# Six-row tiles in four slots, and a first tile loaded whole, in a max-pool-and-subtract kernel

## The chip, the cores and the metric

The kernel runs on one core of one Trainium2 chip. The time is device microseconds (us). Runs of a kernel agree within some 0.03 to 1% (626.60 to 626.78 us in eleven runs of the kernel before), so small differences are judged from repeated rounds beside the kernel before on the same chip.

## The reference

```python
def reference(x):                                   # x: 8 x 64 x 256 x 256 float32
    x_r = x.reshape(B, C, oH, 8, oW, 8)
    pooled = x_r.max(axis=(3, 5))                   # max of each 8 x 8 window
    upsampled = np.repeat(np.repeat(pooled, 8, axis=2), 8, axis=3)
    return (x - upsampled).astype(np.float32)
```

134.22 MB come in, as many go out. A "row" below is 2048 elements (8 lines of 256, 8 KB): the unit that can be pooled alone. There are 128 x 128 of them; a tile of n rows gives each of the 128 partitions n rows in succession.

## The kernel before

One buffer, the ring, holds `SLOTS` tiles of `SIZE` rows. Loads are issued by SyncE (queue q1), stores by ScalarE (queue q10); VectorE pools each tile and subtracts in place. The load of a tile waits for the store of the tile that last had its slot. TensorE only turns "loaded" into one semaphore for the loop.

```python
HEAD, HEAD_OUT = [2, 2], [2, 2]     # first tile: rows per load, rows per store
SIZE, TILES = 5, 24
TAIL = [2, 1, 1]                    # last tile: rows per pooling and store
SLOTS = 5
...
for i in range(len(sizes)):                                     # loads
    slot = slot_of(i)
    if landed[slot]:
        nc.sync.wait_ge(stored[slot], 16 * landed[slot])
    for k, (lo, R) in enumerate(cuts(HEAD if i == 0 else [sizes[i]])):
        nc.sync.dma_start(out=sbuf(i, lo, R), in_=dram(x_rows, i)[:, part]).then_inc(
            first[k] if i == 0 else loaded[slot], 16)
...
for i in range(len(sizes)):                                     # stores
    for lo, R in cuts(HEAD_OUT if i == 0 else TAIL if i == last else [SIZE]):
        ...
        nc.scalar.wait_ge(ready, done)
        nc.scalar.dma_start(out=dram(out_rows, i)[:, part], in_=sbuf(i, lo, R)).then_inc(...)
...
def pool_and_subtract(part, top, R, nth=None):                  # VectorE
    nc.vector.tensor_reduce(out=maxs, in_=..., axis=XY, op=max).then_inc(...)
    ...
    for r in range(R):
        sub = nc.vector.tensor_tensor(out=wins[:, r], in0=wins[:, r], in1=<maxs[:, r] broadcast>, op=subtract)
    sub.then_inc(ready, 1)
```

## Time and profile before

| | before |
|---|---|
| time, median of 3 runs | 626.66 us (626.66 to 626.77) |
| span of the profiled run | 624.8 us |
| bytes | 268.44 MB |
| VectorE busy | 90% |
| DMA engines, loads + stores | 49.9% + 49.7% |
| transfers | 27 loads, 29 stores |

How to read it: two nearly full resources and a clear order between them. The DMA engines are busy all the time; in the steady part VectorE has a gap of about 2.1 us in each turn (a turn is one pass of its loop, one tile), in which it waits for a load. The prediction below shows the lines and the working.

### The profile page before, as it was taken

The numbers are of one execution on the slowest core, as the hardware profiler recorded it, in microseconds if no ns is written. First come the engines' busy times: TensorE is split into PE (matmuls) and PEld (weight loads), VectorE is DVE, ScalarE is ACT, GpSimd is POOL, SyncE is SP. The second block draws the span as 40 slices with busy tenths as digits, with TensorE's granted clock in tenths as the row PEclk, the third lists the DMA queues.
The fourth block names the chain that finished last, engine by engine and source line by source line (L and its number), as shares of the span: only waits on it lengthen the run. The fifth ranks groups of instructions, "written<-read, shape, count | busy, mean of one in ns | idle before, by whom it ended". The sixth has DMA issues, their size and how long they took to land. (4 is left out here: it accounts for less than half of the span.)

```text
span 624.8 us, 557 instructions
## 1 busy us (share of the span) xinstructions
DVE 561.1 (90%) x157; POOL 0.2 (0%) x4
## 2 busy tenths in 40 slices
DVE  4899999999989889898898898898898898988992
POOL 0000000000000000000000000000000000000000
DMA  9999999999999999999999999999999999999998
GB/s 366 406 457 441 420 420 461 420 420 461 420 420 461 420 420 461 420 420 461 420 420 461 420 420 461 420 420 461 420 420 461 420 420 459 422 422 442 450 422 352
DMA packets 8064, 268.44 MB, mean 430 GB/s; under 512 B 896, under 2 KB 896, under 8 KB 896
## 3 DMA queue, kind: packets, MB, share of 16 engines
q1 hardware_dynamic: 3888, 134.22, 49.9%
q10 hardware_dynamic: 4176, 134.22, 49.7%
HBM read 134.22 MB, written 134.22 MB: 430 GB/s over the span
## 5 line engine op out<-in xcount | busy, mean ns | idle before, releaser
L81 DVE TENSOR_REDUCE tops<-ring (+2 forms) x29 | 277.4, 9566 | 47.9 <-DVEq L75 39.6
L96 DVE TENSOR_TENSOR ring<-ring,tops (+1 forms) x128 | 284.4, 2285 | 3.9 <-DVEq L75 3.7
L165 POOL MEMSET const-bfloat16-1.0<- 128x1 bf16 x1 | 0.1, 102 | 0.0
L165 POOL MEMSET const-uint8-127<- 128x1 uint8 x1 | 0.1, 102 | 0.0
L165 POOL MEMSET const-float32-0.0<- 128x1 f32 x1 | 0.1, 99 | 0.2 <-issue 0.2
L165 POOL MEMSET const-float32-1.0<- 128x1 f32 x1 | 0.1, 99 | 0.0
## 6 DMA issues: line engine op xcount, KB each, us to landing
ring<-in_x_dram SPq DMA_DIRECT2D x24, 5120.0 KB, 57.6
out_dram<-ring ACTq DMA_DIRECT2D x24, 5120.0 KB, 40.7
out_dram<-ring ACTq DMA_DIRECT2D x3, 2048.0 KB, 20.9
ring<-in_x_dram SPq DMA_DIRECT2D x2, 2048.0 KB, 9.6
ring<-in_x_dram SPq DMA_DIRECT2D x1, 4096.0 KB, 55.1
out_dram<-ring ACTq DMA_DIRECT2D x2, 1024.0 KB, 11.8
```

The source lines that it names most:

```text
L81: nc.vector.tensor_reduce(out=maxs if R > 1 else maxs[:, 0], in_=(wins.rearrange("p r ph ow pw -> p r ow ph pw") if R > 1 else wins[:, 0]. ...
L96: sub = nc.vector.tensor_tensor(out=wins[:, r], in0=wins[:, r], in1=maxs[:, r].unsqueeze(1).unsqueeze(3).to_broadcast([P, pH, oW, pW]), op ...
L165: nc = _bacc.Bacc("TRN2", target_bir_lowering=False, num_devices=1)
```

## The change

Its intent: fewer, larger transfers, and a simpler head. 24 rows of ring take the place of 25; the first tile of four rows comes in one load, is pooled and stored in halves.

```diff
-HEAD, HEAD_OUT = [2, 2], [2, 2]
-SIZE, TILES = 5, 24
+HEAD, HEAD_OUT = [4], [2, 2]
+SIZE, TILES = 6, 20
 TAIL = [2, 1, 1]
-SLOTS = 5
+SLOTS = 4
...
-        for k, (lo, R) in enumerate(cuts(HEAD)):
-            nc.vector.wait_ge(first[k], 16)
+        for k, (lo, R) in enumerate(cuts(HEAD_OUT)):
+            nc.vector.wait_ge(first[[a + n >= lo + R for a, n in cuts(HEAD)].index(True)], 16)
             pool_and_subtract(sbuf(0, lo, R), top(0, lo, R), R, k + 1)
```

(The rest is the bookkeeping of the same counts.)

More of the change, by code (lines that the diff above doesn't have):

```diff
@@ L127 @@
                 part = slice(lo * ROW, (lo + R) * ROW)
-                done = [sum(HEAD[: k + 1]) for k in range(len(HEAD))].index(lo + R) + 1 if i == 0 else done + 1
+                done += 1
                 nc.scalar.wait_ge(ready, done)
@@ L149 @@
         for k, (lo, R) in enumerate(cuts(TAIL)):
-            pool_and_subtract(sbuf(last, lo, R), top(last, lo, R), R, len(HEAD) + k + 1)
+            pool_and_subtract(sbuf(last, lo, R), top(last, lo, R), R, len(HEAD_OUT) + k + 1)
 _INS = ['x']
```

## The prediction

Its sum came to 626.2 us: from the 626.66 measured, one small term for the nine fewer transfers was taken off, and the rest was rounded towards the change. The 28.9 us near the end still has the term in it.

Three terms in it need their basis. "Packet-wise turns" is the assumption that the 16 engines serve loads and stores in turn, a packet each. The records of the kernel before fit it: while the 256 store packets of 16 KB of the first tile passed (21.69 to 53.35 us), 240 load packets of 40 KB started, 70% of the bytes, where 5/7 is 71%. The 2.6 us beside the bytes are measured; "1.5 of completion" is an estimate of their later part. In the records the last increment of the first load comes 0.35 us after its last packet, that of the first tile's second store 1.80 us after (55.15 us). And the fifth of the five-row loads was released there, at 55.16 us in the trace, where the text reads "near 54" from the wait.

> **What bounds the kernel now.** I read four views in this order: the busy shares, the DMA queues, the stretches, and the waits of the DMA-issuing queues. First the page itself.
>
> ```profile
> span 624.8 us, 557 instructions
> ...
> DVE 561.1 (90%) x157; POOL 0.2 (0%) x4
> ...
> DMA packets 8064, 268.44 MB, mean 430 GB/s; under 512 B 896, under 2 KB 896, under 8 KB 896
> ...
> q1 hardware_dynamic: 3888, 134.22, 49.9%
> q10 hardware_dynamic: 4176, 134.22, 49.7%
> ```
>
> Loads (q1) and stores (q10) take 49.9% and 49.7% of the time of all 16 DMA engines: 99.6% together. VectorE is busy for 90%. So the DMA engines are the bound and VectorE is close behind. Next, the stretches (stretch, its length, busy time of VectorE and of GpSimd, clock, share of the DMA engines, GB/s):
>
> ```profile
> 0.00:2.00 2.00, 0.00 (x0) 0.20 (x4) 1.00 0.16 33
> 2.00:18.00 16.00, 9.61 (x4) 0.00 (x0) 1.00 1.02 422
> 18.00:53.00 35.00, 32.83 (x10) 0.00 (x0) 1.00 0.99 419
> ...
> 185.85:572.96 387.11, 350.69 (x96) 0.00 (x0) 1.00 1.00 434
> ...
> 595.00:613.00 18.00, 17.83 (x8) 0.00 (x0) 1.00 0.96 414
> 613.00:623.00 10.00, 0.00 (x0) 0.00 (x0) 1.00 0.95 403
> 623.00:625.00 2.00, 0.00 (x0) 0.00 (x0) 1.00 0.00 0
> ```
>
> The fourth line is exactly 16 turns of the loop, from the start of one reduce to the start of another. 387.11/16 = 24.194 us a turn, in which five rows per partition come in and five go out: 2 x 5,242,880 B / 24.194 us = 433.4 GB/s. All 268.44 MB at that rate would take 619.4 us; the span is 624.8. Only 5.4 us (0.9%) lie outside the steady rate: about 2 us before the first packet, 1.8 us after the last (nothing moves after 623), and some 1.5 us of slightly lower rate in the head and the tail. The timeline of VectorE shows that it waits in the steady part, not the DMA engines:
>
> ```profile
> 548.89 10.82 DVE L81 TENSOR_REDUCE tops<-ring  x1 [2.17 <-DVEq L75]
> 559.86 11.10 DVE L96 TENSOR_TENSOR ring<-ring,tops  x5 [0.15 <-DVEq L75]
> 572.96 10.82 DVE L81 TENSOR_REDUCE tops<-ring  x1 [2.00 <-DVEq L75]
> ```
>
> Each turn starts with about 2.1 us of waiting for a load. Without that wait a turn takes 21.98 us (the starts at 50.13 and 72.11, early in the same timeline).
>
> [...] The trace: the first load of 2.10 MB was issued at 0.94 and released VectorE at 8.36, 7.4 us; less 4.8 us at 433.4 GB/s leaves 2.6[...].
>
> **The change part by part.**
>
> *Bytes.* None is removed: 134.22 MB in, 134.22 MB out. At a saturated 433.4 GB/s this alone keeps the sum at 619.4 us.
>
> *Number of transfers.* Before: 27 loads (2+24+1) and 29 stores (2+24+3). After: 1+20+1 = 22 loads and 2+20+3 = 25 stores. Nine fewer of 56. Packets are one per partition plus 16 small ones for each transfer (27 x 144 = 3888 and 29 x 144 = 4176, as the queues show), so 3168 and 3600 are to be seen. What is one worth?[...] If transfers were wholly free of cost, 0.
>
> *VectorE.* A reduce costs 2.28 us for one row, 4.41 for two, 10.82 for five: 2.135 a row and about 0.14 fixed. Six rows: 12.95. The 29 reduces become 25 (20 of six rows, three of two, two of one): 276.8 us against 277.4. The 128 subtracts stay. A turn without waiting becomes 21.98 x 6/5 less a share of the fixed part, 26.3 us. A saturated turn becomes 24.194 x 6/5 = 29.03[...]. So VectorE still waits 2.6 to 2.7 us a turn, and gains nothing that reaches the end.
>
> *Head.* The first load is 4.19 MB whole. VectorE starts at 0.94 + 2.6 + 4.19 MB/433.4 = 13.2 us instead of 8.36, and the first store is issued near 22.1 instead of 17.34. This 4.8 us is a delay of VectorE, not of the DMA engines: four more loads of 22 rows in all (4 + 3 x 6) stand in the queue from the start, some 53 us of work at 2.42 us a row (1.049 MB at 433.4).
>
> *Ring.* 24 rows instead of 25, and only three full tiles ahead of the first wait for a store. Is the load queue ever empty with no store at hand? The first store packets are 16 KB, while load packets are 40 KB before and 48 KB after, and by the packet-wise turns the loads get 5/7 and 3/4 of the engines. Check on the kernel before: at 18.3 us, when the first store's packets begin, (18.3 - 1.9)/2.42 = 6.8 rows have come in; the tile's four stored rows then pass beside ten loaded ones, 14 x 2.42 = 33.9, so at 52.2 plus 1.5 of completion the queue of loads is released, near 53.7. The waits of the load queue say:
>
> ```profile
> SPq L113 <- DMA out_dram<-ring: 51.3, 1, 51.3
> ```
>
> This is the view up to 60 us; the wait starts near 3 us after the six first issues, so it ended near 54. The rule holds. After: stores begin near 23.2 us with 8.8 rows in; four stored rows pass beside twelve loaded ones, to 61.9 us, with 20.8 of the 22 rows in. The fifth load is released near 63.5, with about one row left to load and the next six-row store (issued near 57.5) already queued. So the loads nearly run out there, but the engines have store work, and nothing is lost. Carried on by hand, VectorE is behind the loads until about its ninth tile (near 240 us; before it was the seventh, 161.65) and each store lands some 50 us after issue, each load some 35 to 40. Both sums fit the ring: four turns of 29.0 are 116, of which VectorE holds 26.3, so load and store latency and waits must fill 89.7. Before it was 57.6 + 40.7 + 22.
>
> *Tail.* The last four rows are cut as before. When the last load lands (594.3 before: issued 539.2, 55.1 to landing), about 28 us of stores remain, so the end is a drain of stores. VectorE's last 18 us lie beside it. After, a backlog of stores of about four rows (10 us) plus six plus four rows remains, and VectorE finishes its last full tile some 2 to 7 us after that landing. The drain should stay unbroken.
>
> *Sum.* 626.66[...] + 0 (head, under the queue) + 0 (ring) + 0 (tail), and I round towards the change: **626.2 us**.
>
> **The rivals.** (1) *The ring starves.* With four slots both queues could be empty while VectorE works on a six-row tile. Against it: the latencies above sum to three turns, so there is a turn or more of queued work at any time. For it: the load queue gets within some 4 us of empty, and the estimate of the tail leaves only a few us. If 0.5 us were lost in each of 20 turns the time would be 636. Likelier is one gap of 2 to 3 us at the end, 628 to 629. (2) *VectorE becomes the bound.* Its work after the start is 561 us and it starts 4.8 us later; 13.2 + 561 + about 4 of gaps = 578, well before 613. It could be late by some 35 us without effect. Only if its chain fell behind in the drain would it show. (3) *Bigger packets move the rate itself*, 48 KB against 40.[...] (4) *The head gains*, since the first packets are 32 KB, not 16 KB: the stretch 2 to 18 ran at 422 and not 434; all of it back would be 0.4 us.
>
> **Range and chances.** The bound is untouched, and every term is under 1 us unless a queue runs dry.[...] a loss is open-ended, but needs both queues empty. So 624.8 to 628.2 for 8 in 10. Faster by over 2% would need under 614[...]: 0.01. Slower by over 2% needs 12.5 us of idle DMA engines: 0.02. The rest, 0.97, is the same.
>
> **What would show it.** Packets of 3168 and 3600; six-row reduces of 12.95 us; a turn of 28.9 to 29.0 us with 2.6 of waiting; the first reduce near 13.2; the load queue's first wait about 61 us; DMA share of 1.00 in all stretches between 2 and 620; stores that land later than before and loads sooner. Wrong would be a stretch with a share clearly below 1, a turn away from 29.0, or a gap between the last stores.

## The result, and the profile after

The changed kernel takes 626.57 us (median of 6 runs, 626.44 to 627.03); the kernel before took 626.71 in the same rounds. The ratio is 0.9999, with a 95% interval of 0.9986 to 1.0012: the same. Ratios here are the mean time of one kernel's runs over that of the other's of the same rounds, so not quite the ratio of the medians. Executions over 1.5% slower than the fastest of the same kernel are left out of the means.

The page of the changed kernel:

```profile
span 625.3 us, 516 instructions
...
DVE 559.9 (90%) x153; POOL 0.2 (0%) x4
...
q1 hardware_dynamic: 3168, 134.22, 49.8%
q10 hardware_dynamic: 3600, 134.22, 49.6%
...
L81 DVE TENSOR_REDUCE tops<-ring (+2 forms) x25 | 276.8, 11071 | 44.5 <-DVEq L75 31.5
```

The packets are the 3168 and 3600 that were predicted, and the DMA engines are as full as before. The stretches (length, VectorE, GpSimd, clock, DMA share, GB/s):

```profile
186.00:307.00 121.00, 112.55 (x31) 0.00 (x0) 1.00 1.00 432
307.00:428.00 121.00, 109.69 (x29) 0.00 (x0) 1.00 1.00 435
...
595.00:613.00 18.00, 12.61 (x6) 0.00 (x0) 1.00 0.96 413
613.00:623.00 10.00, 0.00 (x0) 0.00 (x0) 1.00 0.93 396
```

The tail is as it was. One steady stretch is a little lower than the others, and VectorE's timeline shows a long turn in it:

```profile
215.03 12.94 DVE L81 TENSOR_REDUCE tops<-ring  x1
...
243.45 12.95 DVE L81 TENSOR_REDUCE tops<-ring  x1 [2.02 <-DVEq L75]
...
273.23 12.95 DVE L81 TENSOR_REDUCE tops<-ring  x1 [3.37 <-DVEq L75]
...
302.07 12.95 DVE L81 TENSOR_REDUCE tops<-ring  x1 [2.43 <-DVEq L75]
...
563.37 12.95 DVE L81 TENSOR_REDUCE tops<-ring  x1 [2.52 <-DVEq L75]
```

From 302.07 to 563.37 are nine turns: 29.03 us each, and the rate before gives 24.194 x 6/5 = 29.03. So the turns show no gain from the larger transfers. (The last seven alone give 28.99; single turns differ by more than that.) The turn that starts at 243.45 took 29.78, and in the packet records some loads between 260 and 280 us took up to 2.44 us in place of 1.81. The first wait of the load queue in the changed kernel:

```profile
SPq L113 <- DMA out_dram<-ring: 62.3, 1, 62.3
```

It was predicted at about 61. On this showing the change does nothing, as foreseen, and its parts should do nothing either. The experiments say otherwise.

### The profile page after: what moved, and what is told of

Same layout as the page of the kernel before. It is cut to its first block, busy times and chain, and to the rows that moved or that the text cites. A ratio compares the mean times of both kernels' runs of the same rounds, so it can differ in the third digit from the quotient of the medians.

```text
span 625.3 us, 516 instructions
## 1 busy us (share of the span) xinstructions
DVE 559.9 (90%) x153; POOL 0.2 (0%) x4
## 3 DMA queue, kind: packets, MB, share of 16 engines
q1 hardware_dynamic: 3168, 134.22, 49.8%
## 5 line engine op out<-in xcount | busy, mean ns | idle before, releaser
L81 DVE TENSOR_REDUCE tops<-ring (+2 forms) x25 | 276.8, 11071 | 44.5 <-DVEq L75 31.5
## 6 DMA issues: line engine op xcount, KB each, us to landing
ring<-in_x_dram SPq DMA_DIRECT2D x20, 6144.0 KB, 32.8
out_dram<-ring ACTq DMA_DIRECT2D x20, 6144.0 KB, 54.7
```

Source lines behind the costliest of these rows:

```text
L81: nc.vector.tensor_reduce(out=maxs if R > 1 else maxs[:, 0], in_=(wins.rearrange("p r ph ow pw -> p r ow ph pw") if R > 1 else wins[:, 0]. ...
```

## The experiments

Twelve kernels ran. Each is an edit of the changed kernel unless said otherwise, with the result correct unless said otherwise. "Theory" in the expectations is: the DMA engines are saturated, so the time follows the bytes, and neither part matters.

| run | time, median (range), us | kernel before, same rounds | ratio, 95% interval |
|---|---|---|---|
| e1_head_only | 710.20 (708.13 to 714.21) | 626.66 | 1.1336 [1.1312, 1.1361] |
| e2_tiles_only | 628.62 (626.05 to 630.18) | 626.66 | 1.0026 [1.0010, 1.0042] |
| e3_load_cut | 652.74 (648.01 to 654.46) | 626.66 | 1.0410 [1.0389, 1.0431] |
| e4_both_cut | 630.45 (629.50 to 630.63) | 626.66 | 1.0057 [1.0044, 1.0070] |
| e5_dve_one | 629.94 (629.85 to 630.16) | 626.69 | 1.0053 [1.0036, 1.0070] |
| e6_dve_two | 672.68 (672.51 to 672.90) | 626.69 | 1.0735 [1.0717, 1.0753] |
| e7_dve_less | 626.62 (626.03 to 628.12) | 626.69 | 0.9996 [0.9979, 1.0013] |
| e8_fewer_bytes | 578.08 (577.81 to 578.22) | 626.69 | 0.9224 [0.9208, 0.9239] |
| e9_slots3 | 654.44 (653.26 to 657.35) | 626.70 | 1.0455 [1.0434, 1.0475] |
| e10_slots2 | 715.74 (714.69 to 716.94) | 626.70 | 1.1414 [1.1398, 1.1431] |
| e11_whole_ends | 627.30 (626.77 to 638.62) | 626.70 | 1.0016 [0.9998, 1.0034] |
| e12_late_store | 708.95 (708.34 to 709.82) | 626.68 | 1.1315 [1.1296, 1.1334] |

### Is VectorE a bound? e5, e6, e7

```diff
+        if nth is None:                 # e5: EXTRA = 1 row, e6: EXTRA = 2 rows; in six-row tiles only
+            nc.vector.tensor_reduce(out=spare, in_=<EXTRA rows of the tile>, axis=XY, op=max)   # result unused
         nc.vector.tensor_reduce(out=maxs, ...
```
```diff
-        for r in range(R):
+        for r in range(R if nth is not None else 3):     # e7: a wrong result on purpose
```

> The changed kernel with one more reduce of one row (2.2 us, result unused) in each six-row tile: 43 us more work for VectorE, a turn without waiting of 28.5 us against the 29.03 of the DMA engines. Theory: the time stays, 626.6 to 628; VectorE's wait falls from 2.6 to about 0.4 us a turn and its busy share rises to 96%. Rival D (VectorE is a bound as well): tens of us slower.

> One more reduce of two rows (4.4 us) in each six-row tile: a turn of 30.75 us, now above the 29.03. Theory: VectorE takes over as the bound; it ends at 30.8 + 20 x 30.75 + 17.9 = 664, and the last store lands some 6 us later: 668 to 672 us, with DMA share below 1 in the steady part. If the time stayed at 627, the theory of a margin of 2.7 us a turn would be wrong.

> Only three of the six subtracts in each six-row tile (a wrong result on purpose): 132 us less work for VectorE, a turn of 19.7 us. Theory: the time stays at 626.6 within 1, all the time saved becomes waiting. Rival D: faster by more than 2%.

With 132 us of VectorE's work taken away the time did not move (626.62). With 43 us more it rose by 3.3 us, to 629.94, over the range of 626.6 to 628. With 86 us more (645.4 us busy) it rose by 46 us; the 672.68 lies just above the range of 668 to 672. The busy time of VectorE in e5 and all that its reduces waited for, and then a turn of e6:

```profile
DVE 602.7 (96%) x173; POOL 0.2 (0%) x4
...
DVE tops L94 <- DMA ring<-in_x_dram: 13.1, 1, 13.1
```

```profile
310.94 12.95 DVE L94 TENSOR_REDUCE tops<-ring  x1
...
337.26 4.41 DVE L84 TENSOR_REDUCE spare<-ring 128x64 f32 x1
341.59 12.94 DVE L94 TENSOR_REDUCE tops<-ring  x1
```

In e6 the next tile starts with no wait at its reduce: VectorE turns in 341.59 - 310.94 = 30.65 us and sets the time. The DMA share was expected to fall below 1 there; it stayed at 0.98 to 1.01 from 53 to 600 us, while the rate fell to between 401 and 424 GB/s. In e5 the expected wait of 0.4 us a turn is missing too: after the first load VectorE never waits for another. It starts at 13 us and is behind the loads at first, so the 43 us of extra work use up the 31.5 us that it waits for later loads in the changed kernel. Its last store is issued at 619.1 us in place of 607.7, and the end comes 3.3 us later. So VectorE is no bound in the changed kernel: the slope has its knee near e5. The 2.6 us are its margin in a steady turn; over the whole run the margin is less than the 2.2 us a turn that e5 added.

### Do the bytes set the time? e8

```diff
-            for lo, R in cuts(HEAD_OUT if i == 0 else TAIL if i == last else [SIZE]):
+            for lo, R in cuts(HEAD_OUT if i == 0 else TAIL if i == last else [SIZE - 1]):
...
-        for r in range(R):
+        for r in range(R if nth is not None else R - 1):
```

> Five of the six rows of each six-row tile are subtracted and stored (a wrong result on purpose): 20.97 MB less to move, 7.8%; VectorE's turn falls to 24.1 us and stays below that of the DMA engines, 26.6. Theory: 20.97 MB / 433.4 GB/s = 48.4 us faster, 578 us within 2. If loads alone (134.22 MB, unchanged) set the time, no change.

578.08 was measured, 48.6 us less, where 48.4 was worked out. The rows that are not stored make the result wrong. The edit also takes work from VectorE; e7 shows that this alone changes nothing. Bytes set the time as long as they move at the steady rate (431 to 437 GB/s in e8 from 53 to 549 us). The next runs show that this condition is not a given.

### What is a transfer worth, and how do the queues share? e3, e4

```diff
+IN = [2, 2, 2]
-            for k, (lo, R) in enumerate(cuts(HEAD if i == 0 else [sizes[i]])):
+            for k, (lo, R) in enumerate(cuts(HEAD if i == 0 else IN if i < last else [sizes[i]])):   # e3 and e4
...
-            for lo, R in cuts(HEAD_OUT if i == 0 else TAIL if i == last else [SIZE]):
+            for k, (lo, R) in enumerate(cuts(HEAD_OUT if i == 0 else TAIL if i == last else IN)):    # e4 alone
```

(The counts in the waits are changed to suit.)

> As the changed kernel, but each load of six rows is three transfers of two rows (16 KB packets): 40 more transfers. Theory: the time stays at 626.6 within 1. If a transfer costs 0.05 us each[...]: +2.0, 628.6. Rule of turns by packets: store packets of the first tile are now as large as load packets, so its two stores pass beside four loaded rows and not twelve, and the first wait of the load queue falls from 62.3 us to about 40; in the steady part whole 48 KB store packets win, stores land in about 25 us (54.7 before) and loads in about 65 (32.8 before). Rule of turns by bytes: none of these move.

> As before, and stores of six rows are three transfers of two rows as well, issued together: 80 more transfers than the changed kernel. Theory: 626.6 within 1. If a transfer costs 0.05 us: +4.0, 630.6. If packet size itself (16 KB and not 48 KB) costs rate, a turn over 29.1 us. By the rule of packet turns the first wait of the load queue is about 40 us as in the kernel with cut loads.

e4, where loads and stores have the same packet size, cost 0.57% with 80 more transfers. Taken against the ratio of the changed kernel (0.9999) that is 0.0058 x 626.7 = 3.6 us, 0.045 us a transfer, near the 0.05 that the expectations tried. The records of single packets give a similar size: 48 KB packets took 37.81 ns a KB (changed kernel), 16 KB packets 38.19 (e4). Three packets of 16 KB take 0.38 x 48 = 18 ns longer than one of 48 KB, which is 9 ns for each of the two more packets. Each added transfer gives each of the 16 engines 8 more packets, 0.07 us.

e3 missed by far: 652.74 and not 626.6 to 628.6. Its queues did what turns by packets would give. The first wait of the load queue fell from 62.3 to 33.3 us (about 40 was expected; e4 had 32.2), and the issues read as follows, with the median time to landing last:

```profile
ring<-in_x_dram SPq DMA_DIRECT2D x60, 2048.0 KB, 59.2
out_dram<-ring ACTq DMA_DIRECT2D x20, 6144.0 KB, 24.6
```

Stores land in 24.6 us (25 expected, 54.7 in the changed kernel), loads in 59.2 (65 expected, 32.8). So the turns by packets are shown, in the steady part too. What was not foreseen is the price, and it shows in the stretches of e3:

```profile
186.00:307.00 121.00, 105.27 (x29) 0.00 (x0) 1.00 1.00 424
...
605.00:632.00 27.00, 26.78 (x12) 0.00 (x0) 1.00 0.59 251
```

There are two losses. The rate in the steady part is 424 GB/s; why is not shown. And at the end the DMA engines stand idle for 41% of 27 us (11 us), while VectorE is busy all the time: with stores that land in 24.6 us and loads in 59.2, no backlog of stores is left when the last load lands, and nothing fills the time of the last two tiles. The changed kernel has the opposite: its stores land late, so a backlog covers the tail.

### The parts of the change alone: e1, e2

```diff
-SIZE, TILES = 6, 20          # e1: the whole head, with tiles of five rows in five slots
-SLOTS = 4
+SIZE, TILES = 5, 24
+SLOTS = 5
```
```diff
-HEAD, HEAD_OUT = [4], [2, 2]      # e2: six-row tiles, with the head of the kernel before
+HEAD, HEAD_OUT = [2, 2], [2, 2]
```

> Tiles of five rows in five slots as before; only the first tile is loaded whole and pooled in halves. Theory (the DMA engines are saturated, so the time follows the bytes): first reduce near 13.1 us instead of 8.4, the same end, 626.7 us within 0.5. Rival A (the head costs what VectorE starts late, and the larger tiles give it back): 4.7 us slower, about 631. Rival B (larger first packets help the head): up to 0.5 us faster, 626.2.

> Six rows in four slots, but the first tile is loaded in two halves as before. Theory: turn of 29.03 us, 626.6 us within 0.5. Rival A (the larger tiles gain what the late head loses): about 622. Rival C (a ring of 24 rows starves a little): above 627.2 with a DMA share below 1 in the steady part.

e2 is 0.26% slower than the kernel before, more than the rounds' noise and near nothing. e1 is 13.4% slower: 83.5 us, from a change that delays one pooling by 4.8 us. No theory had that. Rival A was wrong as well: e2 gains nothing that could make up for it, so the parts do not add up. Their effects are +83.5, +2.0 and together -0.1 us.

Where did 83 us go? The stretch from 53 to 186 us, first of the kernel before, then of e1:

```profile
53.00:186.00 133.00, 128.41 (x37) 0.00 (x0) 1.00 1.00 434
```

```profile
53.00:186.00 133.00, 123.28 (x33) 0.00 (x0) 1.00 1.00 398
```

Look at the last two columns. The DMA share is 1.00 in both, and the rate is 434 and 398 GB/s. A full share says that packets are under way, not how fast they move. In e1 VectorE waits about 6 us in each turn:

```profile
171.77 10.82 DVE L81 TENSOR_REDUCE tops<-ring  x1 [6.01 <-DVEq L75]
...
199.90 10.82 DVE L81 TENSOR_REDUCE tops<-ring  x1 [6.06 <-DVEq L75]
```

A turn takes 199.90 - 171.77 = 28.13 us where it took 24.19. The trace keeps each packet's start and duration. A packet here is one partition's share of one transfer, 40 KB for a five-row tile (the records have 128 such packets for each of the 24 five-row loads). Packets of one kind start close together on the 16 engines. These are the groups of 16 after 66 us, with the shortest and longest packet of each:

```
before   66.65 store  1.51 .. 1.51 us      e1   66.48 store  1.59 .. 2.04 us
         68.16 load   1.51 .. 1.51              68.09 load   1.51 .. 1.51
         69.67 store  1.51 .. 1.51              69.60 store  1.71 .. 2.02
```

In the kernel before, all 16 engines move in step, and every 40 KB packet takes 1.51 us. In e1 the loads still take 1.51, but most stores 1.70 to 1.85, and one in eight, which would be two engines of the 16, some 2.0 us (80 to 260 us). A tile gives an engine 8 packets of each kind. On an engine with 2.0 us a turn takes 8 x (1.51 + 2.0) = 28.1 us, which is the measured turn; at the mean of 1.79 it is 26.4 us, and 10.486 MB / 26.4 us = 397 GB/s, near the measured 398. So the slow engines set the turn, and the others run ahead. The semaphore of each transfer shows this: the trace has the moment at which each of the 16 engines adds its one, and the time from the first to the last of the 16 grows from 0.4 us to 45:

| time from the first engine to the last, for a transfer landing near (within 20 us) | 60 us | 190 us | 320 us | 495 us |
|---|---|---|---|---|
| before (stores) | 0.3 | 0.3 | 0.4 | 0.6 |
| changed kernel (stores) | 0.4 | 0.4 | 1.1 | 1.4 |
| e1 (stores) | 0.4 | 9.7 | 19.6 | 43.0 |

Late in e1 some engines stand idle: from 428 to 549 us the DMA share falls to 0.94, and in the last 24 us it is 0.46. That the fast engines wait there because the ring holds no larger lead is my reading; it was not shown.

### Whole load, or place of the first store? e12

Why should the head do that to the stores of all later tiles? The fast and the slow stores differ in where they stand beside the loads. If the engines go on taking turns by packets, this place is fixed in the head. (A row stands here for one row in every partition, 1.05 MB.) In the kernel before, the first store packets start at 21.69 us, with 7.1 rows loaded, 3.1 past the first tile: 3.1 / 0.625 rows a packet = 5 load packets per engine. Sixteen small store packets per engine pass beside some 16 load packets (256 beside 240 on all engines in the kernel before), so the five-row stores start 21 load packets behind. In e1 the first store packets start at 26.22 us, with 9.0 rows loaded: 5.0 / 0.625 = 8 packets, and 24 behind: three tiles of 8 packets. (With six-row tiles a packet is 0.75 rows; the same sums give 23 for the changed kernel, from 9.25 rows, and 20 for e2, from 7.0.) Then each store packet follows the load of the same partitions three tiles later. The trace's byte counts per direction bear this out:

| bytes loaded less bytes stored | MiB | packets per engine |
|---|---|---|
| before, steady, at the end of each 20 us | 12.50 to 13.75 | 20 to 22 |
| e1, at 60 us | 15.00 | 24 |
| e12, at 60 us | 15.00 | 24 |
| changed kernel, 80 to 280 us | 16.50 to 17.25 | 22 to 23 (of 48 KB) |

The number of bytes between them does not decide alone: from 60 to 540 us e2 was 15.00 to 16.41 MiB ahead and e4 15.20 to 15.58, and their stores took the usual 37.8 ns a KB (48 KB packets) and 38.2 (16 KB packets).

The last kernel puts this to the test. It is the kernel before, with all its transfers, plus 4.8 us of useless work on VectorE ahead of the first pooling:

```diff
+        if nth == 1:
+            nc.vector.tensor_reduce(out=spare[:, : 2 * oW]..., in_=<both rows>, axis=XY, op=max)
+            nc.vector.tensor_reduce(out=spare[:, 2 * oW :], in_=wins[:, 0, 0], axis=X, op=max)
         nc.vector.tensor_reduce(out=maxs, ...
```

> The kernel before (first tile loaded in two halves, tiles of five, five slots, the same 56 transfers of the same sizes), with two reduces of unused result added ahead of the first pooling, about 4.85 us of work for VectorE, so that the first store is issued near 22.2 us as in the kernel with the whole head alone, and not at 17.3. Theory (the place at which the stores fall in step with the loads decides: the first store meets the loads 7.7 packets per engine into the five-row tiles and not 4.5, so that afterwards each store packet directly follows the load packet of the same partitions three tiles later): stores at some 44 ns a KB, 398 GB/s with a DMA share of 1.00 from 53 to 186 us, 700 to 715 us. Rival (the whole first load itself, its 32 KB packets or its one transfer less, breaks the step): 626.7 us within 1, 434 GB/s.

708.95 us, 13.2% slower, with the same 56 transfers of the same sizes as the kernel before. The first store is issued 4.5 us later; the kernel before, then e12:

```profile
17.34 55.23 ACTq L130 DMA_DIRECT2D out_dram<-ring  x4
```

```profile
21.81 31.18 ACTq L144 DMA_DIRECT2D out_dram<-ring  x3
```

Its stretches:

```profile
18.00:53.00 35.00, 34.81 (x12) 0.00 (x0) 1.00 1.02 434
53.00:186.00 133.00, 123.48 (x33) 0.00 (x0) 1.00 1.00 397
186.00:307.00 121.00, 94.96 (x28) 0.00 (x0) 1.00 1.00 397
```

The rate is full until the first five-row store, and 397 GB/s from there on. Stores take about 44.8 ns a KB from 80 to 260 us, loads 37.9. So the whole load is not needed: a delay of the first store is enough. The moment at which the stores first meet the loads decides, in this kernel, between 434 and 397 GB/s for hundreds of us after it. That the meeting of equal partitions is what matters fits the two slow kernels and the counts above, but rests on them alone. Counted in packets at the start of each store packet (the head's load as two), the lead is 24.1 to 25.0 in e1 and e12 from 60 to 360 us, 20.1 to 22.0 in the kernel before and 22.1 to 24.0 in the changed kernel. On this count the changed kernel misses the slow place by about one packet; no run tests that. What in the memories makes such stores slow (the addresses in HBM, 15 MiB apart in the two arrays, or the same partitions of SBUF) no run here separates; it stays open.

### How much ring is needed? e9, e10

```diff
-SLOTS = 4
+SLOTS = 3        # e10: 2
```

> The changed kernel with three slots, a ring of 18 rows. Theory: a slot comes round in 3 x 29.03 = 87.1 us, of which VectorE takes 26.3; 60.8 are left for a load and a store, which need about 61 if both always share the engines, and less where one has them alone. So it just fits: 626.6 to 632. Rival C (24 rows are already at the edge): several per cent slower, 645 or more, with DMA share below 1.

> Two slots, a ring of 12 rows. Theory: the transfers of one slot (store and load, 14.5 us each at the full rate plus about 1.6 each of completion and 1 of issue) stand beside VectorE's work on the other; two turns take some 33 + 26.3 us and more where they overlap: 30 to 33 us a turn, 650 to 700 us, with DMA share of 0.88 to 0.97. If the time stays within 1%, the ring doesn't matter at all.

Both came out slower than expected: 654.44 with three slots (626.6 to 632 expected), 715.74 with two (650 to 700). VectorE's timeline of e9 shows uneven turns:

```profile
264.60 12.95 DVE L81 TENSOR_REDUCE tops<-ring  x1 [1.68 <-DVEq L75]
...
300.84 12.95 DVE L81 TENSOR_REDUCE tops<-ring  x1 [9.83 <-DVEq L75]
```

In its stretches from 53 to 600 us the DMA share is 0.96 to 1.00 and the rate 409 to 422 GB/s. Little time is lost with idle engines; again the packets take longer, here the loads: in the records from 28 to 95 us loads of 48 KB took up to 3.5 us in place of 1.81 where one queue ran dry or came back. In e10 the share is 0.90 to 0.94 and the rate 370 to 386 GB/s, less than that share of 433.4: both effects are there. My sum counted only transfer times at the full rate. (The 1 us of issue and 1.6 of completion in e10's text are an estimate, a split of the 2.6 us measured beside the bytes of the first load.) How much each effect costs was not measured apart. What follows is that the fourth slot of six rows is needed.

### Can both kernels be beaten? e11

```diff
-HEAD, HEAD_OUT = [4], [2, 2]
-TAIL = [2, 1, 1]
+HEAD, HEAD_OUT = [4], [4]
+TAIL = [4]
```

> The changed kernel with the first and the last tile pooled and stored whole (4 rows each), in the search for a faster version: the slower stretches are those with small packets in the head (418 GB/s from 18 to 53 us) and in the tail (396 to 413 from 595 on). If small packets cost rate there: 1 to 2.5 us faster, 624 to 625.5. If those stretches are only the uneven ends of the 16 engines: 626.6 within 0.5. If the later last store opens a gap in the drain: slower, 628 or more.

The fast runs gave 626.77 to 630.66 us; one of 638.62, which is also the profiled one, counts as slow. The interval of the ratio, 0.9998 to 1.0034, holds no gain above 0.02%. No version here beats the two kernels: what a full rate of 433.4 GB/s leaves to gain is 5.4 us in 625, and most of it is the start before the first packet and the end after the last.

## Why the prediction was right

- **The bound and the sum: right.** 626.2 was predicted and 626.57 measured. Taking work from VectorE changed nothing (e7), taking bytes changed the time by their worth (e8, 48.6 for 48.4 us).
- **Number of transfers: a small worth, and no gain that shows.** e4 gives 0.045 us a transfer and the packet records 0.07. The prediction's own term was worked out from a figure that no run here shows. At 9 ns a packet the nine fewer transfers (72 packets per engine) are worth 0.65 us. The median fell by 0.14 us, inside the spread of 0.6 us, and nine steady turns took 29.03 us each, the 24.194 before times 6/5, with no saving. The slow load packets near 260 us may have eaten the gain in the profiled run; that is not shown.
- **VectorE: right.** Reduces of 12.95 us, 276.8 us in all, a wait of about 2.6 us in a steady turn. It caught up with the loads at its ninth six-row tile, at 243.45 (near 240 was said). By e5 its margin over the whole run is smaller than the steady wait suggests.
- **Queues: right, with sizes off.** The first wait was 62.3 for 61 us, although the first store packets start later than the sum had them: at 21.69 us before (18.3 in the sum) and 27.47 after (23.2). Stores land in 54.7 us at the median where "some 50" was said, loads in 32.8 where it was 35 to 40.
- **Tail: right.** ScalarE issued the last store at 607.7 and the drain went on with shares of 0.96 and 0.93, as before.
- **Head: right in its value by luck, and wrong in its reason.** The step said that the 4.8 us delay lies under a queue of 53 us of loads and so costs nothing. In the changed kernel it costs nothing (626.57 with it, 628.62 without it in e2). In the kernel before a delay of 4.5 us costs 82 us (e12), although the queue there is as full. The argument kept account of whether the engines had work, and took the rate of that work as given. In the changed kernel the delay and the six-row packets together put the stores 22 to 23 packets behind the loads, which is harmless; that was not foreseen, and I know of no line of the profile before that warns of it. Two smaller slips: the queue holds four loads of 22 rows in all, not four more, and the 2.6 us beside the bytes are in the trace 1.0 from the issue to the first packet, about 1.2 of first packets slower than 433.4 GB/s, and about 0.35 from the last packet to the last increment.
- **Ring: right for four slots, and closer than I thought.** The rival that starvation costs much got little weight because three turns' worth of latency stood against it. Three slots cost 4.5%, with the engines nearly always busy.

The range was right because the two parts were changed together, and that was luck. Had only the head been changed, the same argument would have been off by 84 us.

## What to carry to other kernels

Read the DMA share and the GB/s together: a share of 1.00 hid the fall from 434 to 398 GB/s (8%; with the idle engines at the end the loss was 13%), and the durations of single packets and the spread of the 16 engines' increments told why. Here the moment of the first store fixed the rate for most of the run: 4.5 us later gave 708.95 us where 626.68 had been (e12). So in a kernel that streams in and out at full rate, try that moment (by a few us of delay or another cut of the first tile) before a change of tile size is judged. When a change has two parts, run each alone even if the sum is as predicted.
